# Gate and up chunks taken in pairs, the first half of their rows by seven block products instead of eight

## The chip, the cores and the metric

The kernel runs on one core of a Trainium2 chip. The metric is device time in microseconds of one execution of the whole program; the time before is the median of three runs. Engines are named as the profile names them: PE (matrix products), PEld (loading of their stationary operand), DVE (vector), ACT (scalar), POOL and SP (here the queue that issues the weight loads).

## The reference

Two transformer-like blocks on 256 tokens of width 2048, all in float32. The change touches the feed-forward part of the second block alone:

```python
D_FF = ((8 * D_MODEL // 3 + 255) // 256) * 256      # 5632
...
        y = _rms(h, norm_ffn_g[i])
        h = h + (jax.nn.silu(y @ w_gate[i]) * (y @ w_up[i])) @ w_down[i]
```

`y` is 256 x 2048, `w_gate` and `w_up` are 2048 x 5632, `w_down` is 5632 x 2048. Everything else (attention branches, mixers, the per-layer embedding) is computed as before.

## The kernel before, in words

All large products run through one stream of weight units. A unit is 4 row tiles of 128 x 512 columns of a weight matrix, 1 MB. For each unit `run_units` (line 224) does four things. SP loads it into `raw` (line 232, three buffers). ACT casts it to `hi` (line 246, fp32r). DVE subtracts, `lo = raw - hi` (line 247). Two units later the unit's function issues its products. `hi` and `lo` have three buffers each, so the cast of a unit waits until PE is through with the unit three places ahead of it.

A product in float32 precision is three passes: `product` (line 215) multiplies the high half of the activations by `lo` (line 217) and by `hi` (line 218), and the low half by `hi` (line 219). The activations are stationary (128 x 128), the weights stream (512 columns). A unit is therefore 4 row tiles x 2 token tiles x 3 passes = 24 products, and both token tiles accumulate in a PSUM bank of 512 columns each (`mm`, pool `psM`, four banks; the other four banks, `at`, serve transposes).

A chunk of 512 columns of `w_gate` or `w_up` has 2048 rows, so four units. The 11 chunks come in groups of 4, 4 and 3 (`ffn_units`, line 1240): for each chunk first the four gate units, then the four up units, and after a group the units of `w_down` for it (16, 16 and 12). After a gate chunk ACT evacuates silu into `sg` (line 1250). After an up chunk DVE multiplies it with `sg` into `act` (line 1256); this adds a task to the background list. One step of that list is issued after each unit (`pump`, line 173), and the step in question, `turn`, transposes `act` on PE (line 260, eight transposes into two banks), casts the banks on ACT (line 276) and subtracts on DVE (line 277). Its first step does nothing, so the transposes stand on PE behind the unit after the one that ended the chunk.

No instruction is moved by a scheduler: each engine runs its instructions in the order in which the program issues them.

Of the kernel before, what the change touches and what calls it, by code (L numbers as in the profile page):

```python
# [17 lines left out]
P = 128  # L18
T = 256
# [12 lines left out]
NRAW = 3  # L32
NHL = 3
# [7 lines left out]
def shape_constants():  # L41
    """Constants that follow from the shapes alone."""
# [42 lines left out]
)  # fmt: skip  # L85
# [48 lines left out]

class Unit:
    def __init__(self, src, nk, ncols, fn):
        self.src, self.nk, self.ncols, self.fn = src, nk, ncols, fn
        self.parts = [nk]  # row tiles that are loaded and split together
        self.beside = lambda k0, k1: None  # runs before a part's load
        self.pre = lambda k0, k1: None  # runs before a part's split  # L140


class Kernel:
# [76 lines left out]

    def run_units(self):
        nc, total = self.nc, len(self.units)
        raw, hl = {}, {}
        for s in range(total + NRAW + NHL):
            if s < total:
                u = self.units[s]
                t = self.pw.tile([P, 4 * CH], F32, tag="raw", name="raw", bufs=NRAW)
                v = t[:, : u.nk * u.ncols].rearrange("p (k n) -> p k n", k=u.nk)
                k = 0
                for n in u.parts:  # L230
                    u.beside(k, k + n)
                    nc.sync.dma_start(out=v[:, k : k + n, :], in_=u.src[:, k : k + n, :])
                    k += n
                raw[s] = v
            j = s - (NRAW - 1)
            if 0 <= j < total:
                u, v = self.units[j], raw.pop(j)
# [3 lines left out]
                vv = v.rearrange("p k n -> p (k n)")  # L241
                k = 0
                for n in u.parts:
# [4 lines left out]
                    k += n  # L248
                hl[j] = [x[:, :c].rearrange("p (k n) -> p k n", k=u.nk) for x in (hi, lo)]
            q = j - (NHL - 1)  # L250
            if 0 <= q < total:
                self.units[q].fn(*hl.pop(q))
                self.pump()

# [7 lines left out]
    def rpow(self, out, s, n):  # L262
        """out = (s / n + EPS) ** -0.5"""
# [5 lines left out]
    def split_ps(self, dst, k0, bank, n, scale=None):  # L269
        """bank [P, n * 256] in PSUM -> tiles k0.. of dst (high, low), each tile times scale(k) [P, 1]."""  # L270
# [15 lines left out]
    def split_sb(self, dst, k0, src, n):  # L286
        """src [P, n, 256] in SBUF -> tiles k0.. of dst."""
# [6 lines left out]
    def turn(self, src, nblk, k0, dst, scale=None):  # L294
        """Transpose token-major src(m) [P, nblk * 128] into tiles k0.. of dst, two tiles a step."""
# [7 lines left out]
    def turn_plain(self, src, dst):  # L303
        """src [P, 2, 512] token-major -> dst [P, 4, 256]"""
# [12 lines left out]
    # ------------------------------------------------------------------  # L317
    def build(self):
        tc, nc, a = self.tc, self.nc, self.a
        with ExitStack() as es:  # L320
# [5 lines left out]
            self.psM = es.enter_context(tc.tile_pool(name="psM", bufs=4, space=PSUM))  # L326
            self.psA = es.enter_context(tc.tile_pool(name="psA", bufs=4, space=PSUM))
# [7 lines left out]
            # constants  # L335
# [115 lines left out]
    def softmax4(self, q, k, scale, bias0, bias1, op):  # L451
        """L[t, slot, 0:128 | 128:384] = exp(logits - max) of the two query tiles; r[:, tile * 4 + slot] = 1 / sum."""
# [27 lines left out]
    def weigh(self, slots, v, vh, out):  # L480
        """out(m) <- sum over s of L[t, s] v[s]; slots of L, heads vh of v."""
# [25 lines left out]
    def normed(self, b):  # L507
        """Evacuation into branch b of y, with the softmax's division."""
# [46 lines left out]
        # index queries  # L555
# [58 lines left out]
        # z  # L614
# [14 lines left out]
        # gates and branches  # L629
# [46 lines left out]
        # w_out, the block's residual and norm  # L676
# [49 lines left out]
    def square(self, pool, src, j):  # L726
        """stat[:, j] = sum of src ** 2"""
# [3 lines left out]
    def total(self, out, src, n):  # L731
        """stat[:, out : out + n] = sums of the n fours from stat[:, src]"""
# [4 lines left out]
    def to_merge(self):  # L737
        """Attention's memory goes; the sums of the branches come."""
# [9 lines left out]
    def to_out(self):  # L748
        """The branches' memory goes; x comes again for the residual."""
# [661 lines left out]
```

## Time and profile before

| what | value |
|---|---|
| three runs | 2131.42, 2131.09, 2128.79 us; median 2131.09 us |
| profiled execution, span from its first to its last instruction | 2125.2 us |
| median less that span | 5.9 us |
| PE busy | 2106.4 us (99% of the span), 9592 instructions |
| DVE busy, ACT busy | 1155.2 us (54%), 913.8 us (43%) |
| gate, up and down products of the second block | about 1282 to 2014 us of the span |

The span lies inside the time that is measured; the profiled execution has no time of its own beside it, so the 5.9 us are taken from the median. A PE row's duration (390 ns) is longer than the distance to the next product, since products overlap; the distance is what counts.

### The profile page before, as it was taken

The page shows a single profiled execution, that of the slowest core. Times are in us where ns is not written, and L with a number is a line of the kernel's source. Part 1 is how long each engine was busy: PE and PEld are TensorE (multiplying, and loading weights), DVE is VectorE, ACT ScalarE, POOL GpSimd, SP SyncE. Part 2 cuts the span into 40 slices and gives each one's busy share as a digit, 9 for nine tenths or more (in the row PEclk, how much of TensorE's full clock was granted, in tenths as well). Part 3 has the DMA queues.
Part 4 walks back from the last instruction along what each step waited for, and adds up shares of the span by engine and source line. Part 5 has one row for each costly group of instructions (what it writes and reads, how often), then busy time and mean ns, then how long its engine had stood idle before and what let it go on. Part 6 is the DMA issues. An engine that isn't in the chain of part 4 may idle for free.

```text
span 2125.2 us, 22828 instructions
## 1 busy us (share of the span) xinstructions
PE 2106.4 (99%) x9592; PEld 1746.1 (82%) x9592; DVE 1155.2 (54%) x1000; ACT 913.8 (43%) x854; POOL 36.6 (2%) x65
## 2 busy tenths in 40 slices
PE   8999999999999999999999999999999999999998
PEld 6888888888888888888888888888888888888886
DVE  6457556544454554565599554445444454444554
ACT  5444444434344344445454444343333433334543
POOL 1100000000000000000100000000000000000000
PEclk9999999999999999999999999999999999999999
DMA  7744354455555555564645445555555555555453
GB/s 264 259 157 179 127 190 159 167 191 194 185 195 192 185 198 187 190 238 178 238 168 189 171 176 223 188 190 186 198 189 188 190 186 198 191 186 192 175 178 129
DMA packets 59127, 401.68 MB, mean 189 GB/s; under 512 B 6788, under 2 KB 7440, under 8 KB 12304
## 3 DMA queue, kind: packets, MB, share of 16 engines
q1 hardware_dynamic: 56592, 388.69, 50.7%
q0 software_dynamic: 2288, 11.43, 1.7%
q8 instruction: 75, 1.23, 0.2%
q14 instruction: 28, 0.23, 0.0%
q10 hardware_dynamic: 144, 0.11, 0.0%
HBM read 398.08 MB, written 4.47 MB: 189 GB/s over the span
## 4 chain that ended last, share of the span: by engine, by line
PE 98%; DMA 1%; DVE 0%; issue 0%; ACT 0%; SPq 0%; ACTq 0%; POOLq 0%; POOL 0%; DVEq 0%
PE mm L217 31%; PE mm L219 31%; PE mm L218 31%; PE at L260 2%; DMA raw<-in_t_w_in_dram 1%; PE at L467 0%; PE at L809 0%; DVE lo L247 0%; PE at L459 0%; PE at L504 0%; PE at L503 0%; PE at L501 0%; PE at L808 0%; DVE part L396 0%; PE at L882 0%
## 5 line engine op out<-in xcount | busy, mean ns | idle before, releaser
L247 DVE TENSOR_TENSOR lo<-raw,hi 128x2048 fp32r<-128x2048 f32 (+2 forms) x375 | 841.1, 2245 | 759.7 <-ACT hi L246 759.6
L246 ACT CAST hi<-raw 128x2048 fp32r<-128x2048 f32 (+2 forms) x375 | 700.9, 1871 | 726.6 <-PE mm L219 661.1
L217 PE MATMUL mm<-lo,xA 128*128 128x512 f32 x2176 | 855.3, 393 | 6.2 <-DVE lo L247 6.2
L219 PE MATMUL mm<-hi,xA 128*128 128x512 f32 x2176 | 848.8, 390 | 0.0
L218 PE MATMUL mm<-hi,xA 128*128 128x512 f32 x2176 | 848.2, 390 | 0.0
L217 PEld LDWEIGHTS mm<-lo,xA 128*128 128x128 f32 x2176 | 409.5, 188 | 92.0 <-DVE lo L247 7.0
L219 PEld LDWEIGHTS mm<-hi,xA 128*128 128x128 f32 x2176 | 409.2, 188 | 85.9
L218 PEld LDWEIGHTS mm<-hi,xA 128*128 128x128 f32 x2176 | 409.6, 188 | 84.1
L217 PE MATMUL mm<-lo,xB 128*128 128x512 f32 x608 | 240.2, 395 | 0.0
L219 PE MATMUL mm<-hi,xB 128*128 128x512 f32 x608 | 238.3, 392 | 0.0
L218 PE MATMUL mm<-hi,xB 128*128 128x512 f32 x608 | 236.9, 390 | 0.0
L219 PEld LDWEIGHTS mm<-hi,xB 128*128 128x128 f32 x608 | 114.2, 188 | 25.9
L218 PEld LDWEIGHTS mm<-hi,xB 128*128 128x128 f32 x608 | 114.2, 188 | 24.6
L217 PEld LDWEIGHTS mm<-lo,xB 128*128 128x128 f32 x608 | 114.3, 188 | 23.2
L1022 DVE SCALAR_TENSOR_TENSOR tr<-tr,cols 128x256 f32<-128x256 f32 x128 | 52.4, 477 | 0.0
L217 PE MATMUL mm<-lo,yT 128*128 128x512 f32 x128 | 50.6, 396 | 0.0
L219 PE MATMUL mm<-hi,yT 128*128 128x512 f32 x128 | 50.5, 395 | 0.0
L218 PE MATMUL mm<-hi,yT 128*128 128x512 f32 x128 | 50.5, 395 | 0.0
L729 ACT ACTIVATE junk<-R 128x512 f32<-128x512 f32 x32 | 20.2, 632 | 52.4 <-DVE R L1268 14.5
L276 ACT CAST xB<-at 128x512 fp32r<-128x512 f32 x30 | 16.1, 590 | 59.9 <-PE at L260 59.9
L640 ACT ACTIVATE sig<-mm,rs 128x512 f32<-128x512 f32 x32 | 21.9, 690 | 42.2 <-PE mm L219 42.2
L281 ACT ACTIVATE xA<-at,cols 128x256 fp32r<-128x256 f32 x48 | 21.4, 472 | 40.3 <-DVE xA L282 20.9
(262 smaller groups left out, 818.0 us busy)
## 6 DMA issues: line engine op xcount, KB each, us to landing
raw<-in_t_w_in_dram SPq DMA_DIRECT2D x164, 1024.0 KB, 4.8
raw<-in_t_w_gate_dram SPq DMA_DIRECT2D x44, 1024.0 KB, 4.7
raw<-in_t_w_up_dram SPq DMA_DIRECT2D x44, 1024.0 KB, 4.8
raw<-in_t_w_down_dram SPq DMA_DIRECT2D x44, 1024.0 KB, 4.8
raw<-in_t_w_out_dram SPq DMA_DIRECT2D x32, 1024.0 KB, 4.8
raw<-in_t_w_branch_dram SPq DMA_DIRECT2D x16, 1024.0 KB, 4.8
raw<-in_t_w_ple_gate_dram SPq DMA_DIRECT2D x16, 1024.0 KB, 4.8
raw<-in_t_w_in_dram SPq DMA_DIRECT2D x6, 512.0 KB, 7.3
```

The lines of the kernel that those rows point to most:

```text
L217: nc.tensor.matmul(ps, xh[:, k, ts], lo, start=first, stop=False)
L218: nc.tensor.matmul(ps, xh[:, k, ts], hi, start=False, stop=False)
L219: nc.tensor.matmul(ps, xl[:, k, ts], hi, start=False, stop=last)
L246: nc.scalar.copy(out=hi[:, o], in_=vv[:, o])
L247: nc.vector.tensor_tensor(out=lo[:, o], in0=vv[:, o], in1=hi[:, o].bitcast(F32), op=ALU.subtract)
L260: self.nc.tensor.transpose(out, in_, self.ident[: in_.shape[0], : in_.shape[0]])
L276: nc.scalar.copy(out=h, in_=bank[:, : n * T])
L281: nc.scalar.activation(out=hi[:, k0 + i, :], in_=b, func=AF.Copy, scale=scale(k0 + i))
L640: nc.scalar.activation(out=s, in_=ps[m], func=AF.Sigmoid, scale=self.r0(m))
L729: self.nc.scalar.activation(out=t, in_=src, func=AF.Square, accum_out=self.stat[:, j : j + 1])
L1022: nc.vector.scalar_tensor_tensor(out=o, in0=i, scalar=s, in1=o, op0=ALU.mult, op1=ALU.add)
```

## The change

The weights of a gate chunk and of the up chunk with the same columns are put side by side. Of the first 1024 rows, the first 512 rows of gate and up are the blocks b11 and b12, the second 512 rows b21 and b22; the two token tiles and the two row halves make four blocks of the activations. Such a 2x2 block product is done with seven block products of 12 passes each instead of eight, for which sums of weight blocks and of activation blocks are multiplied. Rows 1024 to 2047 are multiplied as before. This is done for 10 of the 11 chunk pairs; the first pair is done plainly, and behind it the sums of the activation blocks (`forms`) are made once.

A pair is now eleven units in this order: u1, u5, u6, u3, u7, left 0, u4, left 1, u2, right 0, right 1. The seven u units have 12 products each, the left (rest of gate) and right (rest of up) units 24. Weight sums are made in place in `raw` by DVE (`plus`), before or after the split of a unit. Partial sums go between PSUM banks by ACT copies (b from a, d from b) or into `sn` in SBUF, from which they are added when the up chunk is evacuated. `weave` puts right 0, u1 of the next pair, right 1 in this order and moves the first weight sum of that pair in front of right 1. So a group of n pairs has one first pair and n-1 woven ones. Loads have six `raw` buffers in this part, `psM` five banks and `psA` three; `sg` has two buffers, `act` one.

```diff
+NWIDE = 3
...
+        def plus(pairs):
+            for x, y in pairs:
+                nc.vector.tensor_tensor(out=x.flat(), in0=x.flat(), in1=y.flat(), op=ALU.add)
...
+                plus(u.before)
+                vv = u.load.flat()
...
                     nc.scalar.copy(out=hi[:, o], in_=vv[:, o])
                     nc.vector.tensor_tensor(out=lo[:, o], in0=vv[:, o], in1=hi[:, o].bitcast(F32), op=ALU.subtract)
...
+                plus(u.after)
...
+    def pair_units(self, wl, wr, lhs, forms, evac_l, evac_r, need=None):
...
+        b11, b12, b21, b22 = (Load(src(w, r), 4, CH) for r in range(2) for w in (wl, wr))
...
+        def p1(hi, lo):
+            if need is not None:
+                self.need(need)
+            bank("a")
+            bank("b")
+            product("a", block(0, 0), hi, lo, True)
+            nc.scalar.copy(out=st["b"], in_=st["a"])
+
+        def p5(hi, lo):
+            bank("c")
+            product("c", forms()["F5"], hi, lo, True)
+            keep("s5", "c", 1.0)
+
+        def p6(hi, lo):
+            product("b", forms()["F6"], hi, lo, False)
+            keep("s2", "b", -1.0)
+
+        def p7(hi, lo):
+            product("b", forms()["F7"], hi, lo, False)
+            bank("d")
+            nc.scalar.activation(out=st["d"], in_=st["b"], func=AF.Copy, scale=-1.0)
...
+        u1 = form(b11, p1)
+        u5, u6, u3, u7 = form(b11, p5), form(b11, p6), form(b22, lambda hi, lo: product("c", forms()["F3"], hi, lo, False)), form(b12, p7)
+        u4 = form(b11, lambda hi, lo: product("b", block(1, 1), hi, lo, False))
+        u2 = form(b21, p2)
...
+        u5.before, u5.loads = [(b11, b12)], [b12]
+        u5.after, u5.loads = [(b11, b22)], [b12, b22]
+        u6.before = [(b12, b22)]
+        u7.after, u7.loads = [(b11, b21)], [b21]
+        return [u1, u5, u6, u3, u7, left[0], u4, left[1], u2], right
+
+    def weave(self, pairs):
...
+            if tail:
+                u5 = head[1]
+                tail[1].before, u5.before = u5.before, []
+                tail[1].loads, u5.loads = tail[1].loads + u5.loads[:1], u5.loads[1:]
+                self.units += [tail[0], head[0], tail[1]] + head[1:]
...
+    def forms_of(self, lhs, out):
...
+        for k in (0, 2):
...
+            sub(s5, a21, a22)
+            sub(s7, a11, a21)
+            sub(s6, s5, a11)
+            nc.vector.tensor_tensor(out=s3, in0=s6, in1=a12, op=ALU.add)
+            for src, key in ((s5, "F5"), (s7, "F7"), (s6, "F6"), (s3, "F3")):
+                h, l = (y[:, k : k + 2, :] for y in out[key])
+                nc.scalar.copy(out=h, in_=src)
+                nc.vector.tensor_tensor(out=l, in0=src, in1=h.bitcast(F32), op=ALU.subtract)
...
+    def banks(self, n):
+
+        if n != 4:
+            self.ps.close()
+        self.ps = ExitStack()
+        self.psM = self.ps.enter_context(self.tc.tile_pool(name="psM", bufs=n, space=PSUM))
+        self.psA = self.ps.enter_context(self.tc.tile_pool(name="psA", bufs=8 - n, space=PSUM))
...
+                    *ps, s2, s5 = ps
+                    for m, s in enumerate((s2, s5)):
+                        nc.vector.tensor_tensor(out=s, in0=ps[m], in1=s, op=ALU.add)
+                    ps = s2, s5
```

What stands on DVE, first. Before, in any chunk pair: `act` is the evacuation of the up chunk, `lo` the split of a unit, `xB` the end of the transposes.

```order
L1256 SCALAR_TENSOR_TENSOR act<-mm,rs,sg 128x512 x2
L247 TENSOR_TENSOR lo<-raw,hi 128x2048
L277 TENSOR_TENSOR xB<-at,xB 128x512 x2
L247 TENSOR_TENSOR lo<-raw,hi 128x2048 x7
L1256 SCALAR_TENSOR_TENSOR act<-mm,rs,sg 128x512 x2
```

Now, in a woven pair, from the sum in front of right 1 (`raw<-raw` is a weight sum, `sn<-mm,sn` the adding of kept partial sums):

```order
L277 TENSOR_TENSOR raw<-raw 128x2048
L293 TENSOR_TENSOR lo<-raw,hi 128x2048 x2
L277 TENSOR_TENSOR raw<-raw 128x2048 x2
L293 TENSOR_TENSOR lo<-raw,hi 128x2048
L1446 TENSOR_TENSOR sn<-mm,sn 128x512 x2
L1449 SCALAR_TENSOR_TENSOR act<-sn,rs,sg 128x512 x2
L293 TENSOR_TENSOR lo<-raw,hi 128x2048
L448 TENSOR_TENSOR xB<-at,xB 128x512 x2
L293 TENSOR_TENSOR lo<-raw,hi 128x2048
L277 TENSOR_TENSOR raw<-raw 128x2048
L293 TENSOR_TENSOR lo<-raw,hi 128x2048 x8
```

The two `lo` of the second row are right 1 and u5, the single ones after it u6, u3 and u7, and the last row begins with left 0. Three weight sums and a longer evacuation now stand between u5's split and left 0's.

On PE the same evacuation's transposes are `at<-ident,act`. Before, behind a whole unit (`lo_8710` is the next unit's):

```order
L218 MATMUL mm_8748<-hi_8679,xA_8104 128x512
L219 MATMUL mm_8748<-hi_8679,xA_8104 128x512
L260 MATMUL at_8773<-ident_90,act_8737 128x128 x4
L260 MATMUL at_8780<-ident_90,act_8737 128x128 x4
L217 MATMUL mm_8747<-lo_8710,xA_8104 128x512
L218 MATMUL mm_8747<-hi_8709,xA_8104 128x512
```

Now, in a woven pair (`lo_9032` is u5's, `lo_9052` u6's):

```order
L319 MATMUL mm_9089<-lo_9032,forms_8770 128x512
L319 MATMUL mm_9089<-hi_9031,forms_8770 128x512 x2
L431 MATMUL at_9104<-ident_90,act_9080 128x128 x4
L431 MATMUL at_9111<-ident_90,act_9080 128x128 x4
L319 MATMUL mm_9037<-lo_9052,forms_8770 128x512
L319 MATMUL mm_9037<-hi_9051,forms_8770 128x512 x2
```

Between right 1, which ends the up chunk, and the transposes stands now u5 with 12 products, where a unit of 24 stood.

## Rows read from the trace of the kernel before

**Rows 1.** The page: busy time and share of the span; chain that ended last.

```profile
PE 2106.4 (99%) x9592; PEld 1746.1 (82%) x9592; DVE 1155.2 (54%) x1000; ACT 913.8 (43%) x854; POOL 36.6 (2%) x65
...
PE 98%; DMA 1%; DVE 0%; issue 0%; ACT 0%; SPq 0%; ACTq 0%; POOLq 0%; POOL 0%; DVEq 0%
```

**Rows 2.** Windows: one chunk pair, evacuation to evacuation; busy time, clock, DMA.

```profile
1325.93:1370.28 44.35, 44.35 (x201) 36.83 (x200) 21.04 (x13) 17.53 (x12) 0.00 (x0) 1.00 0.52 190
```

**Rows 3.** Timeline of the pair: start, us, engine, line, op, names.

```profile
1325.93 1.41 DVE L1256 SCALAR_TENSOR_TENSOR act<-mm,rs,sg 128x512 f32<-128x512 f32 x2 [0.59 <-PE mm L219]
...
1331.79 1.03 PE L260 MATMUL at<-ident,act 128*128 128x128 f32 x8
1332.42 1.07 ACT L276 CAST xB<-at 128x512 fp32r<-128x512 f32 x2 [3.96 <-PE at L260]
1332.58 0.48 PE L217 MATMUL mm<-lo,xA 128*128 128x512 f32 x1
1333.04 1.29 DVE L277 TENSOR_TENSOR xB<-at,xB 128x512 fp32r<-128x512 f32 x2 [2.26 <-ACT xB L276]
...
1360.07 1.91 ACT L246 CAST hi<-raw 128x2048 fp32r<-128x2048 f32 x1 [3.53 <-PE mm L219]
1362.02 2.29 DVE L247 TENSOR_TENSOR lo<-raw,hi 128x2048 fp32r<-128x2048 f32 x1 [3.15 <-ACT hi L246]
1365.51 1.91 ACT L246 CAST hi<-raw 128x2048 fp32r<-128x2048 f32 x1 [3.53 <-PE mm L219]
...
1370.28 1.43 DVE L1256 SCALAR_TENSOR_TENSOR act<-mm,rs,sg 128x512 f32<-128x512 f32 x2 [0.52 <-PE mm L219]
1370.76 0.39 PE L217 MATMUL mm<-lo,xA 128*128 128x512 f32 x1
1370.95 1.91 ACT L246 CAST hi<-raw 128x2048 fp32r<-128x2048 f32 x1 [3.53 <-PE mm L219]
```

**Rows 4.** Groups by line and form: busy, mean ns, idle before and its releaser.

```profile
L1250 ACT ACTIVATE sg<-mm,rs 128x512 f32<-128x512 f32 x22 | 15.0, 690 | 31.3 <-PE mm L219 31.3
L1256 DVE SCALAR_TENSOR_TENSOR act<-mm,rs,sg 128x512 f32<-128x512 f32 x22 | 15.7, 750 | 5.8 <-PE mm L219 5.8
L656 DVE TENSOR_TENSOR R<-R,tm 128x512 f32<-128x512 f32 x24 | 16.6, 693 | 0.8
L837 DVE TENSOR_TENSOR bs<-bias,acc 128x1024 f32<-128x1024 f32 x1 | 1.2, 1218 | 0.0
L928 ACT COPY y<-at 128x256 f32<-128x256 f32 x4 | 1.5, 372 | 1.2 <-PE at L504 0.9 <-PE at L501 0.3
L1268 DVE TENSOR_TENSOR R<-R,mm 128x512 f32<-128x512 f32 x24 | 16.5, 688 | 6.7 <-PE mm L219 6.7
```

**Rows 5.** DMA issues: count, KB each, median us to landing.

```profile
raw<-in_t_w_gate_dram SPq DMA_DIRECT2D x44, 1024.0 KB, 4.7
raw<-in_t_w_up_dram SPq DMA_DIRECT2D x44, 1024.0 KB, 4.8
```

**Rows 6.** Timeline where the feed-forward part begins.

```profile
1281.41 1.44 DVE L1202 SCALAR_TENSOR_TENSOR R<-R,rs,mm 128x512 f32<-128x512 f32 x2 [0.25 <-PE mm L219]
...
1281.90 0.39 PE L217 MATMUL mm<-lo,xA 128*128 128x512 f32 x1
```

**Rows 7.** Timeline of a long PE wait early in the program.

```profile
30.48 0.50 PE L401 MATMUL at<-ones,part 128*128 128x1 f32 x4
31.68 1.88 DVE L396 TENSOR_REDUCE part<-sq 128x256 f32<-128x1024 f32 x1
...
33.62 1.33 PE L401 MATMUL at<-ones,part 128*128 128x1 f32 x8 [2.64 <-DVE part L396]
...
36.23 0.63 PE L217 MATMUL mm<-lo,xA 128*128 128x512 f32 x1
36.66 0.63 PE L218 MATMUL mm<-hi,xA 128*128 128x512 f32 x1
```

**Rows 8.** Windows after that wait: PE busy, granted clock, DMA share, GB/s.

```profile
34.00:35.00 1.00, 1.00 (x7) 0.62 0.99 418
35.00:36.00 1.00, 1.00 (x3) 0.50 0.72 287
36.00:37.00 1.00, 1.00 (x4) 0.50 0.31 59
37.00:38.00 1.00, 1.00 (x4) 0.67 0.75 263
38.00:39.00 1.00, 1.00 (x6) 1.00 0.89 360
```

More of the change, by code (lines that the diff above doesn't have):

```diff
@@ L132, in finish, with __init__, flat @@
             self.step()
+class Load:
+    def __init__(self, src, nk, ncols):
+        self.src, self.nk, self.ncols = src, nk, ncols
+        self.v = None
+    def flat(self):
+        return self.v.rearrange("p k n -> p (k n)")
 class Unit:
-    def __init__(self, src, nk, ncols, fn):
-        self.src, self.nk, self.ncols, self.fn = src, nk, ncols, fn
+    def __init__(self, src, nk, ncols, fn, load=None):
+        self.nk, self.ncols, self.fn = nk, ncols, fn
+        self.load = load or Load(src, nk, ncols)
+        self.loads = [] if src is None else [self.load]
         self.parts = [nk]
@@ L140, in __init__ @@
         self.pre = lambda k0, k1: None
+        self.before, self.after = [], []
 class Kernel:
@@ L219, in product, with plan_loads @@
         nc.tensor.matmul(ps, xl[:, k, ts], hi, start=False, stop=last)
+    def plan_loads(self):
+        items = self.units
+        for i, u in enumerate(items):
+            for x in u.loads:
+                x.need, x.unit = i, u
+            u.load.last = i
+            for pair in u.before + u.after:
+                for x in pair:
+                    x.last = i
+        wide0, wide1 = items.index(self.wide[0]) + NHL - 1, items.index(self.wide[1])
+        free = [-1] * NRAW + [wide0] * NWIDE
+        loads = [x for u in items for x in u.loads]
+        for x in loads:
+            ok = [n for n in range(NRAW + NWIDE) if n < NRAW or x.last < wide1]
+            x.slot = min(ok, key=lambda n: (free[n], n))
+            x.after = free[x.slot]
+            assert x.after < x.need
+            free[x.slot] = x.last
+        return loads
@@ L221, in run_units, with fetch @@
     def run_units(self):
         nc, total = self.nc, len(self.units)
[L223 to L228, printed above, removed]
+        loads, hl = self.plan_loads(), {}
+        def fetch(j):
+            while loads and loads[0].after <= j:
+                x = loads.pop(0)
+                pool = self.pw if x.slot < NRAW else self.pr
+                t = pool.tile([P, 4 * CH], F32, tag=f"raw{x.slot}", name="raw", bufs=1)
+                x.v = t[:, : x.nk * x.ncols].rearrange("p (k n) -> p k n", k=x.nk)
@@ L229, in run_units @@
                 k = 0
-                for n in u.parts:
-                    u.beside(k, k + n)
-                    nc.sync.dma_start(out=v[:, k : k + n, :], in_=u.src[:, k : k + n, :])
+                for n in x.unit.parts if x.unit.load is x else [x.nk]:
+                    if x.unit.load is x:
+                        x.unit.beside(k, k + n)
+                    nc.sync.dma_start(out=x.v[:, k : k + n, :], in_=x.src[:, k : k + n, :])
                     k += n
-                raw[s] = v
@@ L235, in run_units @@
-            j = s - (NRAW - 1)
-            if 0 <= j < total:
-                u, v = self.units[j], raw.pop(j)
+        def plus(pairs):
+            for x, y in pairs:
+                nc.vector.tensor_tensor(out=x.flat(), in0=x.flat(), in1=y.flat(), op=ALU.add)
+        fetch(-1)
+        for j in range(total + NHL - 1):
+            if j < total:
+                u = self.units[j]
                 c = u.nk * u.ncols
@@ L248, in run_units, with product, bank, keep @@
                     k += n
+                plus(u.after)
                 hl[j] = [x[:, :c].rearrange("p (k n) -> p k n", k=u.nk) for x in (hi, lo)]
             q = j - (NHL - 1)
-            if 0 <= q < total:
+            if q >= 0:
                 self.units[q].fn(*hl.pop(q))
                 self.pump()
+            fetch(j)
+    def pair_units(self, wl, wr, lhs, forms, evac_l, evac_r, need=None):
+        nc = self.nc
+        src = lambda w, r: w[r].rearrange("p (k n) -> p k n", n=CH)
+        st = {}
+        b11, b12, b21, b22 = (Load(src(w, r), 4, CH) for r in range(2) for w in (wl, wr))
+        def product(key, x, hi, lo, first):
+            xh, xl = x
+            for k in range(4):
+                for i, (x_, w_) in enumerate(((xh, lo), (xh, hi), (xl, hi))):
+                    nc.tensor.matmul(
+                        st[key], x_[:, k, :], w_[:, k, :], start=first and k + i == 0, stop=k == 3 and i == 2, skip_group_check=True
+                    )
+        def bank(key):
+            st[key] = self.psM.tile([P, CH], F32, tag="mm", name="mm")
+        def keep(key, src, scale):
+            st[key] = self.p5.tile([P, CH], F32, tag="sn", name="sn", bufs=2)
+            nc.scalar.activation(out=st[key], in_=st[src], func=AF.Copy, scale=scale)
+        def block(r, m):
+            return [x[:, 4 * r : 4 * r + 4, m * P : m * P + P] for x in lhs()]
+        def p1(hi, lo):
[16 more added lines that the diff above has]
+            nc.scalar.activation(out=st["d"], in_=st["b"], func=AF.Copy, scale=-1.0)
+        def p2(hi, lo):
+            product("a", block(1, 0), hi, lo, False)
+            evac_l((st["a"], st["b"]))
+        def rest(w, r, keys, then=None):
+            def fn(hi, lo):
+                for m, key in enumerate(keys):
+                    product(key, block(r, m), hi, lo, False)
+                if then is not None:
+                    then()
+            return Unit(src(w, r), 4, CH, fn)
+        form = lambda load, fn: Unit(None, 4, CH, fn, load)
+        u1 = form(b11, p1)
+        u5, u6, u3, u7 = form(b11, p5), form(b11, p6), form(b22, lambda hi, lo: product("c", forms()["F3"], hi, lo, False)), form(b12, p7)
+        u4 = form(b11, lambda hi, lo: product("b", block(1, 1), hi, lo, False))
+        u2 = form(b21, p2)
+        left = [rest(wl, r, "ab") for r in (2, 3)]
+        right = [rest(wr, 2, "cd"), rest(wr, 3, "cd", lambda: evac_r(st["c"], st["d"], st["s2"], st["s5"]))]
+        u1.loads = [b11]
+        u5.before, u5.loads = [(b11, b12)], [b12]
[3 more added lines that the diff above has]
+        return [u1, u5, u6, u3, u7, left[0], u4, left[1], u2], right
```

87 lines of the change are left out of this document (63 added, 24 removed).

## The prediction

> **What bounds the kernel now.** I read the page first: PE is busy for 99% of the span, and 98% of the chain that ended last is PE [rows 1]. So products set the time, and a product less is time less as long as PE does not have to wait for something else. Then the window of one chunk pair, from one up evacuation to the next: 44.35 us, PE busy throughout at full granted clock, DVE busy for 21.04 us and ACT for 17.53 us [rows 2]. Third, the timeline of that pair [rows 3]. The casts start at 1360.07 and 1365.51: a unit of 24 products takes PE 5.44 us, so 12 take 2.72 us and eight transposes 0.79 us (1331.79 to 1332.58). The reader should see that each cast starts when PE ends a unit (0.19 us after the next unit's first product, 1370.76 to 1370.95) and not when data arrives: a cast waits for the unit three places ahead to give back its buffer. From there the split goes cast 1.91, 0.04 between, `lo` 2.29, so 4.2 us, and PE has two units in hand, 10.88 us. The cover is 6.6 us. The change halves most units and puts more DVE work under the same cover; the question is whether it still fits.
>
> **What the change removes.** Each of 10 pairs has 12 products fewer: 10 x 2.72 = 27.2 us of PE.
>
> **What it adds.** Per pair: three more splits (three casts, three `lo`), four weight sums, four ACT copies of 512 columns, two DVE adds. A weight sum has no row before. It is a float32 addition of 2048 columns on DVE; the additions of 512 and 1024 columns took 693 and 1218 ns [rows 4], 1.025 ns a column, so 2048 come to 2.27 us, and the `lo` of that width takes 2.29 [rows 3]. I take 2.29. Two multiplications of 0.75 us [rows 4] back to back take 1.43 [rows 3], 0.07 less than their sum; this overlap gives the lower bound: 0.07 less at each of some nine joints of a pair. The upper bound is the sum as it stands. The adds of 512 take 0.69 [rows 4], two of them 1.32 by that overlap. The copies cost ACT 0.69 each, as the silu evacuation [rows 4]; they lie beside product units that do not use the bank. DVE then has 15 x 2.29 and about 4 us of small work, 38.4 us, in a pair for which PE needs 41.5: by shares it fits. By order it does not.
>
> **A woven pair, step by step.** Clock 0 is the end of right 0. u5's cast waits for it (three buffers: right 0, u1, right 1, u5). Cast 0.19 to 2.10; `lo` of u5 to 4.43; weight sum b11 to 6.72; weight sum b12 to 9.01; `lo` of u6 to 11.30 (its cast ran under the second sum); two adds and two multiplications of the up evacuation, 1.32 + 1.42, to 14.04. Only now can the transposes start, and they stand on PE in front of u6: at 14.14, with 0.1 us from DVE to PE (0.06 us in the early wait: 31.68 + 1.88 to 33.62 [rows 7]). PE was there after u1, right 1 and u5, at 2.72 + 5.44 + 2.72 = 10.88. It waits 3.26 us.
>
> Behind it: transposes to 14.93, u6, u3, u7 to 23.09. DVE meanwhile: `lo` of u3 to 16.33, the two `xB` (1.29) to 17.62; u7's cast stands on ACT behind the two casts of the transposes (they begin 0.63 after the transposes and take 1.07 [rows 3]) and ends at 17.75; `lo` of u7 to 20.08; weight sum b11 + b21 to 22.37; and only then `lo` of left 0, whose DVE work is queued behind that sum, to 24.66. PE starts left 0 at 24.76 and has waited another 1.67 us. From left 0 on (left 0, u4, left 1, u2, right 0: 21.76 us) units are long and DVE gets ahead. The loop closes at 24.76 + 21.76 = 46.5 us, against 44.35 before [rows 2]: the waits, 4.93 us, are more than the 2.72 us saved. Seven pairs are woven (2, 3 and 2): 34.5 us of waits.
>
> **First pairs of groups two and three.** Here u5 has all sums itself, and its cast waits for the first of them. From the end of the third-last down unit: cast and `lo` of u1 to 4.43, sum 6.72, cast to 8.67, `lo` of u5 11.00, sum 13.29, the down evacuation's two additions (688 ns each [rows 4]) 14.61, sum 16.90, `lo` of u6 19.19. PE is at u6 at 16.32 and waits 2.97; then `lo` u3, `lo` u7, sum, `lo` left 0 (9.16) against three units (8.16): 1.00 more. 4.0 us each, 8 us.
>
> **The first pair of group one**, with the forms. Clock 0 is the end of the plain pair. DVE comes out of u5's split and sum at 2.41, evacuates `act` to 3.83; the transposes now stand directly behind the plain pair, without a unit between, and wait 3.9 us. u1 ends at 7.44. DVE: sum 6.12, `lo` u6 8.41, `xB` 9.70, then the forms twice: two additions of 512 (1.32), four of 256, a cast of 256 columns (372 ns [rows 4]), four subtractions of 256. The 256-wide one has no row; the line through 693 and 1218 gives 0.43. So 5.17 us a half, the end at 20.04. u5's second half needs the form that is done at 18.75; u5 ends at 20.21, u6 at 22.93, u3 25.65, u7 28.37. ACT casts u7 only after u5's copy, by 23.00, so `lo` u7 ends at 25.33, the sum 27.62, `lo` left 0 29.91. Left 0 starts at 30.0 where transposes and five units end at 14.4 without a wait: 15.6 us.
>
> **Where the part begins**, the five banks are a new pool, and the first gate product has to wait for the last DVE reader of the old one: 1281.41 + 1.44 + 0.1 against 1281.90 [rows 6], 1.05 us.
>
> **At no cost:** the loads. They are as many as before, each issued at least four units ahead, 10.9 us or more, and land in 4.8 us [rows 5]; if that cover went, PE would wait up to 4.8 us per load. The `forms` overwrite a block of `yT2` that nobody reads after the plain pair.
>
> **Sum.** Waits 34.5 + 8.0 + 15.6 + 1.05 = 59.1; saved 27.2; net +31.9. On the span 2125.2 + 31.9 = 2157.1; with the 5.9 us that the median lies above it, 2163. Lower bound of the steps by the DVE overlap (0.07 x 9 x 7, and 2 us in the rest): 6 us less, 2157. Forms at 0.37 instead of 0.43 take another 1.
>
> **The clock.** After PE had waited 2.64 us between a few small products [rows 7], the granted clock stood at 0.50 for about three microseconds, the lower of the two levels, 1.2 GHz; products came every 0.43 us instead of 0.227 [rows 7, 8]. One such fall costs some 7 products x 0.2 = 1.5 us. The new waits of 3.0 to 3.3 us are longer than that one. In the forecast I count nothing, because the slow products would be u6, u3 and u7, behind which PE waits 1.67 us for left 0 anyway.
> The Trainium skill, "TensorE: Matmul & The Clock Gate", section "HAM oscillation — how this bites in real kernels", says that idle gaps between bursts of products put the gate back to half rate again and again, so that the penalty is paid at every gap. By it each of the waits would bring a fall, the trace's one long wait agrees, and the sum would grow by what is not covered.
>
> **Rivals.**
> 1. *The slow clock is not covered.* The fall sets in late, so that the half rate lasts into left 0: 1.5 us at each of nine waits of 3 us, +13.5, 2176. For it: in the early wait dense products ended before 30.5 and the clock fell only between 34 and 35 [rows 7, 8], when the wait was over and products ran again. Against: left 0 begins some 14 us after the wait does. The rule above speaks for this rival.
> 2. *Faster: DVE's chain keeps up.* If the chain from right 0 to the transposes is at most 10.9 us long instead of 14.1, no wait stands in the loop, and 27.2 us less the once-only 15.6 and 1.05 remain: 2120.5. For it: DVE's and ACT's shares in rows 2. Against: it needs 3.2 us less, more than a whole weight sum, and no row shows DVE adding float32 at another rate.
> 3. *Half of the waits.* The transposes' wait is as computed, left 0's and the first pairs' are not there, and the overlap is at its bound: waits 22.8 - 4.4, the forms' 15.6 less its own left 0 wait of 1.6, and 1.05, so 33.4; net +6, 2137; with still less it is no change. For it: left 0's wait rests on the longest sum of small steps.
> That the change does not do what it says I rule out: PE has 12 products in the u units.
>
> **Chances.** Forecast 0.65, rival 1 0.17, rival 3 0.10, rival 2 0.08. A measurement tells about 0.2% (4 us) from no change. Faster: rival 2, 0.07. Same: half of rival 3's lower side and an edge of rival 2, 0.05. Slower 0.88. The range reaches from the overlap bound of 2157 some way towards rival 3, 2146, and to rival 1 and a little more, 2180; the forecast's own is 2155 to 2170.
>
> **What would show it.** In the changed trace: PE waits at `at` for DVE `act` seven times for about 3.3 us and once for 3.9; PE waits at `mm` for DVE `lo`, about 1.7 us at left 0, 3 us at u6 in two first pairs; one wait near 10 us in the first pair at the forms; woven loops of 46.5 us; `raw<-raw` 40 times at 2.29 us; PE's chain share below 98%; granted clock 0.5 behind the long waits. Wrong would be: loops near 42 us (rival 2), a sum much shorter than 2.29 us, left 0 slow at half clock (rival 1).

## The result, and the profile after

The changed kernel takes 2158.3 us, median of four runs (2156.91 to 2159.55), the kernel before 2130.05 us (2128.79 to 2131.42): ratio 1.0133, 95% interval 1.0119 to 1.0148. It is 28.3 us slower; 31.9 were forecast, and 2158.3 lies inside the range. The profiled span grew from 2125.2 to 2156.7 us.

The page after: busy times, the chain that ended last, the group of the weight sums.

```profile
PE 2105.4 (98%) x9472; PEld 1736.0 (80%) x9472; DVE 1328.0 (62%) x1110; ACT 992.5 (46%) x932; POOL 36.6 (2%) x65
...
PE 90%; DVE 6%; issue 2%; ACT 2%; DMA 1%; SPq 0%; ACTq 0%; POOLq 0%; POOL 0%; DVEq 0%
...
L277 DVE TENSOR_TENSOR raw<-raw 128x2048 f32<-128x2048 f32 x40 | 91.0, 2288 | 0.7
```

Against [rows 1], PE has 120 instructions fewer and is busy for as long as before, since some products ran slowly; its busy share hides the new gaps. The chain tells it: PE's share fell from 98 to 90%, and DVE and ACT stand in it with 8%. What PE waited for (total us, times, longest):

```profile
PE at L431 <- DVE act L1449: 19.9, 15, 3.1
PE mm L319 <- DVE lo L293: 7.0, 7, 2.5
...
PE mm L319 <- ACT forms L422: 4.4, 2, 2.5
...
PE mm L233 <- DVE R L1381: 0.8, 1, 0.8
```

L431 are the transposes, L319 the products of the pairs. None of these waits is in the kernel before. Where the time lies is read from marks that both kernels have: the first gate product and the first `w_down` evacuation of each group. The evacuations, before and after:

```profile
1481.96 1.37 DVE L1268 TENSOR_TENSOR R<-R,mm 128x512 f32<-128x512 f32 x2 [0.57 <-PE mm L219]
...
1747.52 1.38 DVE L1268 TENSOR_TENSOR R<-R,mm 128x512 f32<-128x512 f32 x2 [0.57 <-PE mm L219]
...
1963.19 1.37 DVE L1268 TENSOR_TENSOR R<-R,mm 128x512 f32<-128x512 f32 x2 [0.57 <-PE mm L219]
```

```profile
1284.75 0.50 PE L233 MATMUL mm<-lo,xA 128*128 128x512 f32 x1 [0.84 <-DVE R L1381]
...
1500.08 1.38 DVE L1461 TENSOR_TENSOR R<-R,mm 128x512 f32<-128x512 f32 x2 [0.57 <-PE mm L235]
...
1773.00 1.37 DVE L1461 TENSOR_TENSOR R<-R,mm 128x512 f32<-128x512 f32 x2 [0.58 <-PE mm L235]
...
1994.77 1.38 DVE L1461 TENSOR_TENSOR R<-R,mm 128x512 f32<-128x512 f32 x2 [0.57 <-PE mm L235]
```

With the first product before at 1281.90 [rows 6], group one takes 215.33 instead of 200.06 us (+15.3), group two 272.92 instead of 265.56 (+7.4), group three 221.77 instead of 215.67 (+6.1). That and 0.8 at the start make +29.6. Another 2.0 us of the span lie ahead of the part, in code that did not change.

A woven pair on DVE, from u5's split to left 0's:

```profile
1381.61 2.29 DVE L293 TENSOR_TENSOR lo<-raw,hi 128x2048 fp32r<-128x2048 f32 x1 [1.38 <-ACT hi L292]
1383.94 4.49 DVE L277 TENSOR_TENSOR raw<-raw 128x2048 f32<-128x2048 f32 x2
1388.35 2.28 DVE L293 TENSOR_TENSOR lo<-raw,hi 128x2048 fp32r<-128x2048 f32 x1
1390.55 1.28 DVE L1446 TENSOR_TENSOR sn<-mm,sn 128x512 f32<-128x512 f32 x2
1391.75 1.41 DVE L1449 SCALAR_TENSOR_TENSOR act<-sn,rs,sg 128x512 f32<-128x512 f32 x2
1393.08 2.28 DVE L293 TENSOR_TENSOR lo<-raw,hi 128x2048 fp32r<-128x2048 f32 x1
1395.28 1.28 DVE L448 TENSOR_TENSOR xB<-at,xB 128x512 fp32r<-128x512 f32 x2
1396.70 2.29 DVE L293 TENSOR_TENSOR lo<-raw,hi 128x2048 fp32r<-128x2048 f32 x1
1398.91 2.28 DVE L277 TENSOR_TENSOR raw<-raw 128x2048 f32<-128x2048 f32 x1
1401.11 4.53 DVE L293 TENSOR_TENSOR lo<-raw,hi 128x2048 fp32r<-128x2048 f32 x2
```

The reader should see that DVE has hardly any idle time from 1383.9 to 1405.6 (0.14 us in front of u7's split, at 1396.70). And PE in the same pair: u1 (whose first product marks the end of right 0), the last of u5, the transposes, u6, left 0.

```profile
1379.42 0.39 PE L319 MATMUL mm<-lo,xA 128*128 128x512 f32 x1
...
1389.92 0.63 PE L319 MATMUL mm<-hi,forms 128*128 128x512 f32 x2
1392.64 0.30 PE L431 MATMUL at<-ident,act 128*128 128x128 f32 x1 [2.09 <-DVE act L1449]
1393.21 0.98 PE L431 MATMUL at<-ident,act 128*128 128x128 f32 x7 [0.27 <-DVE act L1449]
...
1394.93 0.63 PE L319 MATMUL mm<-lo,forms 128*128 128x512 f32 x1
1395.36 1.05 PE L319 MATMUL mm<-hi,forms 128*128 128x512 f32 x2
1396.21 0.63 PE L319 MATMUL mm<-lo,forms 128*128 128x512 f32 x1
...
1403.88 0.39 PE L319 MATMUL mm<-lo,xA 128*128 128x512 f32 x1
```

PE stands still until `act` is there. From 1394.93 three products take 1.28 us instead of 0.68: the granted clock is at the lower of its two levels, 0.50 of full speed. Left 0 then starts without a wait, 0.5 us after its `lo` was done at 1403.4 (the first of the two in the last DVE row): the slow products used up the wait that was forecast there. These three products and the whole pair as windows, in the columns of [rows 2] (length; busy time of PE, PEld, DVE, ACT and POOL with the number of instructions; granted clock; DMA share; GB/s). Over the pair the clock is 0.96:

```profile
1394.93:1396.21 1.28, 1.28 (x4) 0.99 (x3) 1.28 (x3) 1.28 (x1) 0.00 (x0) 0.50 0.00 0
1391.75:1437.95 46.20, 43.85 (x188) 35.72 (x188) 37.51 (x22) 25.16 (x19) 0.00 (x0) 0.96 0.50 182
```

### The profile page after: what moved, and what is told of

It is laid out like the page before. It is cut to its first block, busy times and chain, and to the rows that moved or that the text cites. A ratio compares the mean times of both kernels' runs of the same rounds, so it can differ in the third digit from the quotient of the medians.

```text
span 2156.7 us, 22848 instructions
## 1 busy us (share of the span) xinstructions
PE 2105.4 (98%) x9472; PEld 1736.0 (80%) x9472; DVE 1328.0 (62%) x1110; ACT 992.5 (46%) x932; POOL 36.6 (2%) x65
## 4 chain that ended last, share of the span: by engine, by line
PE 90%; DVE 6%; issue 2%; ACT 2%; DMA 1%; SPq 0%; ACTq 0%; POOLq 0%; POOL 0%; DVEq 0%
PE mm L233 24%; PE mm L235 24%; PE mm L234 24%; PE mm L319 14%; DVE lo L293 3%; PE at L431 2%; DVE raw L277 1%; ACT hi L292 1%; DVE act L1449 0%; PE at L646 0%; DVE sn L1446 0%; PE at L988 0%; DMA raw<-in_t_w_in_dram 0%; DMA y<-in_l_xT_dram 0%; PE at L638 0%
## 5 line engine op out<-in xcount | busy, mean ns | idle before, releaser
L293 DVE TENSOR_TENSOR lo<-raw,hi 128x2048 fp32r<-128x2048 f32 (+3 forms) x405 | 908.5, 2248 | 640.2 <-ACT hi L292 639.5
L292 ACT CAST hi<-raw 128x2048 fp32r<-128x2048 f32 (+3 forms) x405 | 756.9, 1873 | 668.6 <-PE mm L235 438.1
L233 PE MATMUL mm<-lo,xA 128*128 128x512 f32 x1536 | 606.8, 395 | 6.8 <-DVE lo L293 6.0
L235 PE MATMUL mm<-hi,xA 128*128 128x512 f32 x1536 | 600.8, 391 | 0.0
L234 PE MATMUL mm<-hi,xA 128*128 128x512 f32 x1536 | 600.2, 391 | 0.0
L233 PEld LDWEIGHTS mm<-lo,xA 128*128 128x128 f32 x1536 | 289.8, 189 | 68.5 <-DVE lo L293 6.8
L235 PEld LDWEIGHTS mm<-hi,xA 128*128 128x128 f32 x1536 | 289.7, 189 | 60.9
L234 PEld LDWEIGHTS mm<-hi,xA 128*128 128x128 f32 x1536 | 290.1, 189 | 59.7
L319 PE MATMUL mm<-hi,xA 128*128 128x512 f32 x960 | 296.2, 390 | 0.0
L319 PEld LDWEIGHTS mm<-hi,xA 128*128 128x128 f32 x960 | 180.6, 188 | 37.6
L319 PE MATMUL mm<-lo,xA 128*128 128x512 f32 x480 | 188.0, 392 | 2.1 <-DVE lo L293 2.1
L319 PEld LDWEIGHTS mm<-lo,xA 128*128 128x128 f32 x480 | 90.4, 188 | 22.9 <-DVE lo L293 4.2
L277 DVE TENSOR_TENSOR raw<-raw 128x2048 f32<-128x2048 f32 x40 | 91.0, 2288 | 0.7
L319 PE MATMUL mm<-hi,forms 128*128 128x512 f32 x240 | 83.5, 431 | 0.6 <-DVE forms L423 0.6
L319 PE MATMUL mm<-lo,forms 128*128 128x512 f32 x120 | 53.4, 445 | 9.3 <-DVE lo L293 4.9
L319 PEld LDWEIGHTS mm<-hi,forms 128*128 128x128 f32 x240 | 51.0, 212 | 13.4 <-DVE forms L423 1.5
```

The source lines that it names most:

```text
L233: nc.tensor.matmul(ps, xh[:, k, ts], lo, start=first, stop=False)
L234: nc.tensor.matmul(ps, xh[:, k, ts], hi, start=False, stop=False)
L235: nc.tensor.matmul(ps, xl[:, k, ts], hi, start=False, stop=last)
L277: nc.vector.tensor_tensor(out=x.flat(), in0=x.flat(), in1=y.flat(), op=ALU.add)
L292: nc.scalar.copy(out=hi[:, o], in_=vv[:, o])
L293: nc.vector.tensor_tensor(out=lo[:, o], in0=vv[:, o], in1=hi[:, o].bitcast(F32), op=ALU.subtract)
```

## The experiments

The theory tested: not the amount of DVE's work but its order makes PE wait. Short units follow each other where DVE has most to do. Rivals: the products and bank copies themselves, the place of the transposes, the slow clock, the amount of DVE's work. Beside these runs the kernel before had medians of 2129.46 to 2130.07 us; what a run gains or loses against the changed kernel is taken from 2158.3 us.

**Without the sums (e1).**

```diff
-                nc.vector.tensor_tensor(out=x.flat(), in0=x.flat(), in1=y.flat(), op=ALU.add)
+                pass
```

> The changed kernel without its 40 weight sums on VectorE (so the forms of the weights are not summed and the output is not the reference's); loads, splits, products and evacuations are as they were. Theory (the order of VectorE's work sets the end of each pair: split of u5, two sums, split of u6 and the evacuation stand in front of the transposes, and one more sum in front of left 0's split): the chain in front of the transposes is 4.6 us shorter and the wait there was 2.4 us, so no wait is left in the woven pairs; they take about 41.6 us instead of 46.2, the two first pairs of groups two and three lose their waits of 2.5 us and what follows, the forms' wait stays but for some 2 us. Time 2112 to 2122 us, and PE waits for `act` no more than once. Rival A (the products themselves: copies between banks, the kept partial sums and the transposes' place hold PE up, whatever VectorE has to do): woven pairs of 44 us or more, 2140 to 2155. Rival B (the two adds of the evacuation and the transposes' place are enough for a wait): a wait of 2 us at the transposes stays, 2130 to 2140.

Measured: 2112.29 us (2111.57 to 2114.01), ratio to before 0.9921 (0.9906 to 0.9936). The waits for `act` are all but gone (0.6 us in all, of 19.9):

```profile
PE mm L319 <- ACT forms L422: 4.0, 2, 3.0
...
PE at L431 <- DVE act L1449: 0.6, 2, 0.3
```

Transposes of woven pairs follow each other by 41.9 us (1383.39, 1425.34, 1467.22). So 91 us of DVE work cost 46 us, and products, copies and transposes by themselves hold up next to nothing: rivals A and B fall.

**The sums as dead work in the kernel before (e8).**

```diff
+                if u.extra:
+                    nc.vector.tensor_tensor(out=vv, in0=vv, in1=vv, op=ALU.add)
```

> The kernel before with VectorE's 40 weight sums added as dead work: in the ten pairs that the change touches, every second split is followed by one addition of 128x2048 in place (nobody reads it), four per pair. No product less, no other order. Theory (a sum costs nothing where each unit has 24 products, since a unit of 5.4 us leaves room for a split and a sum, 4.6 us; it costs where units of 2.7 us follow each other): no change against before, 2127 to 2133 us, although VectorE is then as busy as in the changed kernel to within a few us. Rival F (the amount of VectorE's work, or its reading and writing beside the other engines and the loads, slows the rest): 2135 us or more.

Measured: 2129.19 us against 2129.46, ratio 0.9998 (0.9989 to 1.0007). The window of [rows 2] in this kernel:

```profile
1325.93:1370.28 44.35, 44.35 (x201) 36.83 (x200) 30.08 (x17) 17.54 (x12) 0.00 (x0) 1.00 0.52 190
```

DVE 9.04 us more, the pair 44.35 us as before. Forty sums of the same size are free under units of 5.44 us, where nobody waits for their results; in the changed kernel, with units of 2.72 us that need them, they cost 46 us. DVE is not as busy here as the expectation has it: 1246 us in all against 1328 in the changed kernel, 30.08 us in the pair against 37.51. So this run does not yet settle rival F at the changed kernel's amount; e4 does.

**Transposes one unit later (e2).**

```diff
+        for _ in range(wait):
             yield
...
+                wait = min(len(ps), 2)
```

> The changed kernel with the transposes of `act` one unit later in the woven pairs (behind u6 instead of behind u5), nothing else. Theory: the wait for `act` goes (PE has 2.7 us more), but VectorE's chain to left 0's split is as long as before, so PE waits there, or at u6 and u3, for what it waited at the transposes: 2155 to 2161 us, waits at `at` nearly gone, waits for `lo` grown to about 25 us in total. Rival B (the transposes' place is the cause of the wait): woven pairs shorter by 2.4 us and fewer falls of the granted clock, 2130 to 2142 us. Rival C (the slow clock behind the transposes' wait costs time of its own): by as many falls as go, 1.7 us each, so 2145 to 2150.

Measured: 2163.14 us (2159.05 to 2164.32), ratio 1.0155 (1.0140 to 1.0170): no gain, and above the 2155 to 2161 expected. In the pair shown above:

```profile
1392.65 1.03 PE L431 MATMUL at<-ident,act 128*128 128x128 f32 x8
1394.56 0.47 PE L319 MATMUL mm<-lo,forms 128*128 128x512 f32 x1 [0.88 <-ACT sn L328]
...
1402.27 0.50 PE L319 MATMUL mm<-lo,xA 128*128 128x512 f32 x1 [1.98 <-DVE lo L293]
```

The wait moved to left 0, as the theory says. The 0.88 is a wait at u3, which the theory did not have. The profile puts it down to the copy of a kept sum on ACT (1393.93 to 1394.53), but u3's split on DVE ended only 0.1 us before that copy, at 1394.42. The time above the range is the clock's. This pair and one of group two, with nearly the same waits:

```profile
1392.65:1438.33 45.68, 42.70 (x190) 34.51 (x189) 37.29 (x22) 24.86 (x20) 0.00 (x0) 1.00 0.50 184
1619.71:1667.01 47.30, 44.38 (x189) 35.71 (x188) 37.29 (x22) 24.86 (x20) 0.00 (x0) 0.96 0.48 178
```

Where the clock stays up, the pair is shorter than the changed kernel's 46.20 us. In six of the seven pairs it falls behind the wait at left 0, and the loops measured with a fall take 47.3 to 47.6 us: PE waits for nothing more there, so the slow products cost their full 1.6 us. In the changed kernel the fall comes in front of left 0, and the next experiment asks what it costs there.

**The clock alone (e7).**

```diff
+            b = self.bank()
+            for _ in range(9):
+                self.nc.tensor.matmul(b, fill[:, 0, 0:P], fill[:, 0:2, :].rearrange("p k t -> p (k t)"), start=True, stop=True)
```

> The changed kernel with nine extra products of 512 columns, into a bank that nobody reads, on PE in front of the transposes of the woven pairs, where it waited 2.1 us: 63 products more, 14.3 us of PE that was idle. It takes the idle time away and with it the fall of the granted clock, and leaves VectorE's chain as it is. Theory (the slow products lie in time that PE would wait for left 0 anyway): the falls behind the transposes go (no more than four falls in this part instead of ten), PE waits 1 to 1.7 us for `lo` at left 0 instead, and the time stays: 2153 to 2160 us. Rival C (the slow clock costs its own 1.7 us at each of seven falls): 2144 to 2149 us.

Measured: 2156.07 us (2153.3 to 2157.09), ratio 1.0123 (1.0109 to 1.0136). The nine products fill the gap, the clock stays up, and the wait comes back at left 0; the window runs from one first transpose to the next:

```profile
1392.33 2.23 PE L892 MATMUL at<-xA 128*128 128x512 f32 x9
...
1405.40 0.50 PE L319 MATMUL mm<-lo,xA 128*128 128x512 f32 x1 [0.97 <-DVE lo L293]
```

```profile
1394.58:1440.50 45.92, 44.67 (x197) 36.20 (x198) 37.42 (x22) 25.07 (x20) 0.00 (x0) 1.00 0.51 183
```

At full clock the pair takes 45.92 us instead of 46.20: DVE's order sets it. 14 us of extra products cost nothing, and in this order the slow clock costs 2.2 us in all by the medians (the two kernels' runs just overlap), not 1.7 at each of seven waits.

**Forms earlier (e3, e6).** In e3 three of the four forms are made beside the plain pair's up products, the fourth behind it; in e6 all four. The lines that both share:

```diff
+                    def less(ps):
+                        gate_evac(ps)
+                        self.add(self.forms_of(self.yT2, forms), name="forms")
...
                     def more(ps):
                         up_evac(0, 0)(ps)
-                        self.add(self.forms_of(self.yT2, forms), name="forms")
```

> The changed kernel with three of the four forms of the activations made during the plain pair's up products (in other buffers), the fourth behind the plain pair while u1, u5, u6 and u3 run; woven pairs as they were. Theory: the forms are a one-time cost on the path, because they stand between the plain pair and u5; beside the plain pair VectorE has more than 20 us to spare, so the wait at the forms (some 5 us, and what the splits behind it lose) goes: 11 to 14 us less, 2144 to 2148 us. Rival D (the first pair of group one is bound by its sums and splits anyway): 2 to 5 us less, 2153 to 2157. Rival E (early forms hold up the splits of the plain up units): no gain.

> The changed kernel with all four forms made during the plain pair's up products; order of units and sums as in the changed kernel. In e3, with the fourth form late, PE still waited 4.0 us for it at u7 and 2.8 us at u6, and the gain was 3.7 us instead of 11 to 14. If the late form alone took the gain away: 4 us less than e3's 2154.6, about 2150 or below. If the first pair is bound by its own sums and splits (chain of u6, u3, u7 and left 0 as in the first pairs of groups two and three): the wait moves to left 0, 2152 to 2155.

Measured: e3 2154.57 us (2153.89 to 2155.36), ratio 1.0119 (1.0103 to 1.0134); e6 2148.01 us (2147.11 to 2149.98), ratio 1.0088 (1.0072 to 1.0103). e3 gains 3.7 us, in rival D's range; two new waits take the rest:

```profile
PE mm L319 <- ACT xA L437: 4.0, 1, 4.0
PE mm L319 <- ACT xB L460: 2.8, 1, 2.8
```

The first is u7 at the late fourth form; the expectation had counted it as free. In e6 it is gone, and the other, at u6, stays with 3.1 us. The profile names a cast on ACT there, but u6's own split, which stands behind the second weight sum, ended only 0.06 us before that cast (1337.43 and 1337.49): it is the first pair's own sums. So the forms' place is worth 10.3 us.

**Another order of units and sums (e4).**

```diff
...
+        u1.loads, u1.after = [b11, b12], [(b11, b12)]
+        u5.before, u5.loads = [(b12, b22)], [b22]
+        u5.after = [(b11, b22)]
+        u2.loads = [b21]
+        u4.before = [(b11, b21)]
-        return [u1, u5, u6, u3, u7, left[0], u4, left[1], u2], right
+        return [u1, u5, u2, u6, u3, u7, left[0], left[1], u4], right
...
-                self.units += [tail[0], head[0], tail[1]] + head[1:]
+                self.units += [head[0], tail[0], tail[1]] + head[1:]
```

`weave` still moves u5's sum in front of right 1, and the gate chunk's evacuation goes from u2 to u4, now the last of its units.

> The changed kernel with another order of the same units and sums: in a woven pair u1 stands in front of right 0, u2 between u5 and u6, u4 at the end, and the sums are spread (the first two in front of the splits of right 0 and right 1, the last one in front of u4's split); in first pairs likewise. Nothing is left out or added. Theory (it is the order, and not the amount, of VectorE's work that makes PE wait): VectorE gets two long units in front of u5's chain, and three of the four waits go: woven pairs 41.6 to 42 us, 2114 to 2126 us with the forms still on the path. Rival F (VectorE's amount of work binds: 38 us of 41.6, with what the queue costs): woven pairs of 44 us or more, 2138 or more. Rival G (loads now come too late for the earlier sums, since slots are held longer): waits for `raw` of 1 to 4 us in each woven pair, 2130 to 2145.

Measured: 2117.22 us (2116.07 to 2118.84), ratio 0.9946 (0.9929 to 0.9962). The same instructions, 41 us faster than the changed kernel. A woven pair:

```profile
1386.16:1428.20 42.04, 42.04 (x190) 34.75 (x189) 37.65 (x22) 25.08 (x19) 0.00 (x0) 1.00 0.55 200
```

DVE is busy for 37.65 us, as much as in the changed kernel's 37.51, and PE no longer waits in the pair. Rivals F and G fall.

**The two halves of e4 (e9 sums, e10 units).** e9 keeps the units' order and moves two sums; e10 has e4's order with the sums where they were.

```diff
-        u6.before = [(b12, b22)]
-        u7.after, u7.loads = [(b11, b21)], [b21]
+        u5.before, u5.loads = [(b11, b12), (b12, b22)], [b12, b22]
+        left[0].after, left[0].loads = [(b11, b21)], left[0].loads + [b21]
```

> Half of e4: the units stand in the changed kernel's order, and only the sums are moved (the second one in front of right 1's split with the first, the last one behind left 0's split). By the step-by-step count of VectorE's queue: in front of the transposes one sum less stands behind right 0, but the splits of right 1 and u5 start later for it, so PE still waits some 2.7 us at the transposes; left 0's wait of 1 to 1.7 us moves to u4, at 0.7 us. About 8 us less than the changed kernel, 2147 to 2153 us. Rival (moving sums is what made e4): 2120 to 2130.

> The other half of e4: the units in e4's order, the sums at the places of the changed kernel (the first in front of right 1's split, the second in front of u6's split, the last behind u7's split). By the same count: no wait is left at the transposes, but u6 waits 1.1 us, u3 0.8 and left 0 1.3 in each woven pair, so about 11 us less than the changed kernel, 2144 to 2150 us. Rival (the units' order alone made e4): 2117 to 2125.

Measured: e9 2166.74 us (2165.14 to 2168.97), ratio 1.0171 (1.0154 to 1.0188), slower where 8 us less were expected; e10 2138.23 us (2136.91 to 2138.41), ratio 1.0039 (1.0024 to 1.0054), 6 us below its range. Why e9 missed, ACT and then PE:

```profile
1407.92 1.90 ACT L292 CAST hi<-raw 128x2048 fp32r<-128x2048 f32 x1 [4.64 <-DVE raw L277]
1409.73 0.58 ACT L353 ACTIVATE mm<-mm 128x512 f32<-128x512 f32 x1
```

```profile
1410.36 0.50 PE L319 MATMUL mm<-lo,xA 128*128 128x512 f32 x1 [1.25 <-ACT mm L353]
```

u4's cast stands on ACT and waits 4.64 us for the sum that is now directly in front of it; the bank copy behind u7 is queued behind that cast, and left 0 waits for the copy, whose source is the bank of its second token tile. There are ten such waits, 12.5 us in all; e9 lies 13.7 us above its range. The count had looked at DVE's queue alone. So neither half makes e4: the units' order brings 20 us, moving these sums alone costs 8, both together (with the last sum a unit later still) bring 41.

**Both (e5): e4's order, all forms early.**

> The reordered kernel of the run before (e4) with all four forms made during the plain pair's up products, the fourth in buffers of its own. Theory: what is left on the path in e4 is the once-only part (3.3 us at the first transposes, 2.5 us at the forms and the slow clock behind both, with the splits queued behind the forms): 7 to 10 us less than e4's 2117, 2106 to 2111 us, that is 19 to 24 us faster than before, of 27.2 us of products saved. Rival: as in e3 the first pair is bound by its own sums anyway, so 1 to 4 us less than e4, 2113 to 2116.

Measured: 2110.35 us (2109.19 to 2110.50), ratio to before 0.9909 (0.9895 to 0.9922): faster than both kernels. A woven pair:

```profile
1380.09:1422.11 42.02, 42.02 (x190) 34.66 (x188) 37.58 (x22) 25.09 (x19) 0.00 (x0) 1.00 0.54 200
```

In the chain that ended last PE has 97%, where the changed kernel had 90. Of the 27.2 us of products, 19.1 arrive; of the 19 to 24 us expected this is the least.

## Why the prediction was right, step by step

**Sign, mechanism and size were right.** By groups, its terms give +17.3 (forms 15.6, two woven pairs at 4.93, less three times 2.72), +7.9 and +5.7; measured +15.3, +7.4 and +6.1. The start of the part was forecast at 1.05 and shows a wait of 0.84. The saving is there but for a small part: without the sums, pairs come at 41.9 us, where 44.35 - 2.72 is 41.6.

**The woven pair.** From the end of right 0 (1379.42), forecast and measured: `lo` of u5 done 4.43 and 4.48; both sums 9.01 and 9.01; `lo` of u6 11.30 and 11.21; `act` 14.04 and 13.74; first transpose 14.14 and 13.22; `lo` of left 0 24.66 and 23.98; loop 46.5 and 46.2 to 46.9. Two sizes were off. Neighbours on DVE overlap by some 0.08 us, which the prediction had kept as its lower bound. And the transposes do not wait for both multiplications: the first four need one token tile only. So that wait is 2.36 us (2.63 in one pair), not 3.26; it occurs seven times, as forecast. The loop came out near 46.5 all the same, because at the slow clock u6 took 4.42 us (1393.95 to 1398.37) instead of 2.72: the wait forecast at left 0, 1.67 us, was replaced by slow products of the same size.

**Left 0** hardly waits (0.94 us at most, 1.67 forecast), as slow products came first. That is the step in which the clock was counted at nothing, and it is borne out twice. In six of the seven woven pairs the clock fell behind the wait for `act` (0.70 from 1392.64 to 1398.40). In one it did not, after the same wait, and there left 0 waits longest:

```profile
1712.44:1718.20 5.76, 5.49 (x27) 4.51 (x28) 5.61 (x5) 4.81 (x6) 0.00 (x0) 1.00 0.36 107
```

```profile
1723.26 0.50 PE L319 MATMUL mm<-lo,xA 128*128 128x512 f32 x1 [0.94 <-DVE lo L293]
```

And in e7, without the falls, left 0 waits about 1 us in such pairs, and the four loops that can be compared are 0.3 to 0.7 us shorter. Rival 1's mechanism does exist: e2 shows it, where the fall sets in at left 0. The Trainium skill, "TensorE: Matmul & The Clock Gate", section "HAM oscillation — how this bites in real kernels", has the penalty paid at every gap. The falls came as it says at six of the seven gaps; of the penalty most was covered here.

**First pairs of groups two and three.** u6 waits 2.47 and left 0 not at all; 2.97 and 1.00 were forecast. Here too the clock fell behind the wait (0.61 and 0.63 in the 3.4 us from u6's first product), so that slow products stand where a wait was counted.

**The first pair of group one** is the term that was mis-sized: left 0 starts at 1357.53, 28.1 us after the plain pair (1329.5), not 30.0. Its transposes wait 3.10 us, where 3.9 were forecast. Transposes, u5 and left 0:

```profile
1332.58 0.33 PE L431 MATMUL at<-ident,act 128*128 128x128 f32 x1 [3.10 <-DVE act L1449]
...
1340.94 0.50 PE L319 MATMUL mm<-lo,forms 128*128 128x512 f32 x1 [2.46 <-ACT forms L422]
...
1345.07 0.50 PE L319 MATMUL mm<-lo,forms 128*128 128x512 f32 x1 [1.91 <-ACT forms L422]
...
1357.53 0.50 PE L319 MATMUL mm<-lo,xA 128*128 128x512 f32 x1 [0.39 <-DVE lo L293]
```

A half of the forms took 4.14 us on DVE (1338.70 to 1342.84), not 5.17: some 0.6 us of that is overlap again, and 0.4 is the cast, which the prediction put into DVE's chain but ACT did beside DVE's next additions (1340.48 to 1340.89). Instead of "one wait near 10 us" there are two at u5, 2.8 and 2.2 us with the small ones behind them. That sign of the list was wrong: the prediction's own steps already had two waits there, 10 us together. The two measured come to 5.0, since the forms were shorter and PE, at the slow clock, came to u5 at 1338.48, 9.0 us after the plain pair instead of 7.4. Of the 13.7 us that are left of the term (28.1 less 14.4), e6 shows 10.3 to be the forms' place; a wait of 3.1 us at u6 stays without them.

**The 5.9 us** between span and median are no fixed distance, and the close agreement of the spans (2157.1 forecast, 2156.7 measured) is luck. In every run that lists both, time and span lie 1.7 to 1.8 us apart, and the spans of the kernel before are 2125.7 to 2129.8 us: the profiled one of 2125.2 was an execution some 4 us faster than the median. Fair comparisons are the medians, +28.3 us against 31.9, and the part between its marks, +29.6 against the 31.95 of its terms. The 2.0 us ahead of the part, in code that did not change, hide that difference in the span.

**Loads** cost nothing, as forecast: none of PE's new waits is for one.

Still open: of each woven pair's 2.72 us even e5 gets 2.33 (42.02 against 44.35). Of the remaining 0.4 its trace gives 0.3 to u5, u6, u3 and u7, whose 48 products take 11.17 us instead of 10.88 (u6, u3 and u7 from 1383.73 to 1392.10, u5 from 1419.31 to 1422.11); why these come more slowly no run tells. e10 did better than its count because the waits are shorter than counted: 3.2 us for `lo` in each of seven woven pairs, so 22.4, were expected, and all of them, first pairs included, come to 12.2:

```profile
PE mm L319 <- DVE lo L293: 12.2, 22, 1.3
```

Which step of that count was too long was not followed up.

## What to carry to other kernels

A product saved on the bounding engine counts only if the work that feeds it keeps its cover: work out the cover (units in hand times the length of a unit) at the shortest run of units, not over the stage. Where short units and extra work fall together, reorder before giving up: the same instructions took 2158 us in one order and 2117 in another. And follow every in-order queue, not only the busiest: a cast that waits on ACT holds the copy behind it. A fall of the clock is to be priced by what stands behind it: about 0.3 to 0.7 us where PE would soon have waited anyway, 1.6 us where it would not (e2).

## What was unexpected of the hardware

Unchanged code in front of the changed part did not take the same time in each execution: the first gate product stood at 1281.76 us in e1 and at 1286.69 in e7, though both run the same program up to there. Stages are therefore compared from a mark inside the trace. Nor did the same wait always bring the same clock: after 2.36 us of waiting for `act` it fell in one woven pair and stayed up in another of the same trace. And two DVE operations of 128x2048 in a row took 4.49 us where one takes 2.29, an overlap of 0.09 us; two of 512 columns (`sn`) took 1.28 where one takes 0.684, also 0.09. So it does not grow with their size.
